# Storing Strassen weight differences from GpSimd, loading two units' partial sums a step earlier, and issuing the first loads from two engines

## The chip, the cores and the metric

The kernel runs on one core of one Trainium2 chip. The metric is the device time of one execution in microseconds; a kernel's time is the median of its timed runs. Besides these there is one profiled execution, from which a trace is taken; its span goes from the first to the last instruction.

## The reference, cut to what matters

One hybrid encoder layer with a final norm, for two sequences with the same weights, "sample" (1024 tokens) and "prompt" (512 tokens), all in float32, model width 2048:

```
h = rms_norm(x, norm_g)
z = h @ w_in                                  # 2048 x 5632
c_val, c_glu, c_gate, q, k, v, a_gate = split(z)
conv_out = silu(layer_norm(depthwise31(c_val * sigmoid(c_glu)))) @ w_pw * silu(c_gate)
attn_out = banded_sink_attention(rope(q), rope(k), v, sink) * silu(a_gate)
x = x + concat(conv_out, attn_out) @ w_out    # 2048 x 2048
y = rms_norm(x, final_norm_g)
```

The change touches how `h @ w_in` begins for the sample, and how `concat(...) @ w_out` is done for the sample. What is computed stays the same.

## The kernel before, in words

**Matrix products.** [...] The two big projections of the sample are made with a Strassen-Winograd scheme: a `Unit` (line 94) makes a 2 x 2 block product from seven block products P1 to P7 instead of eight. Each of the seven is a step of 12 matmuls of 128 x 512 (four blocks of the sum by three passes). Their weight operands are blocks of the raw weights and differences of them, made by VectorE in `make1` and `less2` (lines 145 to 167, through `sub`, line 142). Their token operands are made in the same way from the activations; they are kept in `e.T`. Products gather in three PSUM banks: P6, P7 and P4 go on in the bank of P1, P3 in that of P5. So before P6 starts, the bank's value after P1 has to be taken out (`tap`); the same holds for P7 after P6, for P4 after P7 and for P3 after P5.

**Order of the stages.** The sample's `w_in` products (four groups of units, two halves of the inner dimension each), attention and convolution beside the prompt's `w_in` products (plain `Job`s, line 669), the pointwise products, then the sample's output projection: `over[0]` and `over[1]` (line 2063), eight units of kind `Onto` (line 271) each, for the two halves of the inner dimension. The prompt's end follows (`LastPost`). It makes its output projection by the same scheme with weights and tokens exchanged, and uses the weight differences that the sample's units made: each of the 16 units has `u.sums` (line 1367) and stores its differences P5, P6, P4 (lines 155 to 157) and P7 (lines 165 and 166) to the DRAM arrays `wsum_P5` and so on. Such a store moves 256 KB: 128 partitions of 4 pieces of 512 bytes. The prompt's end reads them back (line 1658).

**Sums in the output projection.** An `Onto` unit adds its products onto a sum that is already in DRAM: the transposed input `xT_s` in `over[0]`, the first half's `part_out` in `over[1]`. `begin` (line 282) takes a buffer with `E()` (line 477: in turn from `g` and `u`, four buffers each) and has SyncE load the sum into it; `tap` (line 301) has VectorE add the PSUM bank onto it at line 304; when the block is complete it is stored, to `part_out` from `over[0]` and to `y_d` (line 1375) from `over[1]`. The four sums are (0,0) for P1, (0,1) for P6, (1,1) for P5 and (1,0) for P4. `product` (line 291) begins the sum of the step that lies `ahead` steps on, and past the last step the (0,0) of the next unit (`self.next`). `open` begins the unit's own (0,0) if nobody has. `ahead` is 2; for the first two units of `over[1]` it is 0 (lines 2088 and 2089), and the first of the two has no `next`.

**Two units side by side.** `grouped` (line 1877) puts the first two units of `over[1]` into one item: `run` (line 640) makes a step of the one and then a step of the other. The second unit (`side`) uses PSUM banks `s`, `s`, `pt`, takes an `a` buffer for its second raw weights, and a `g` buffer for its P6 difference. This lengthens the time in which the token operands of the new half (`switch`, line 1932) are loaded and made.

**What sets the order on an engine.** The program is written in the order of the steps. When it is built, a planner of the framework gives each engine its instructions in a fixed list: it follows the order of the program, with lines under `urgently` or `high_priority` moved forward, and takes what it expects to be ready by estimated times. On the chip each engine and each issuing queue then goes strictly through its list: an instruction that waits holds all behind it. SyncE issues nearly all DMAs: weights (`raw` buffers, three), sums, tokens, and all stores that go through `Encoder.store` (line 503). GpSimd issues only what is written with `nc.gpsimd.dma_start` (lines 268 and 501), and ScalarE eight stores of gates (line 983). DMAs of SyncE go round eight semaphores, so one waits for the eighth before it.

**The head.** `constants` (line 561) has SyncE load `norm_g` first. `first` (line 1886) then loads the first unit's weights in four pieces and the first half of the eight rows `x[k]` of the transposed input in the order of use, and the second halves after that. 20 products of ones (`warm`, line 554) keep TensorE at work until the first operands are there. A row becomes an operand at lines 514 and 515, which need `norm_g`.

Of the kernel before, what the change touches and what calls it, by code (L numbers as in the profile page):

```python
# [7 lines left out]
F32 = mybir.dt.float32  # L8
# [5 lines left out]
P = 128  # L14
D = 2048
ND = D // P
# [17 lines left out]
W = 512  # L34
# [59 lines left out]
class Unit:  # L94
# [50 lines left out]
    def make1(self):  # L145

        if self.late:
            t2 = self.e.G([HALF, P]) if self.side or not self.total else self.e.A([HALF, P], F32)
        else:
            t2 = self.e.PT("p", NP, [HALF, P])  # L150
        r1, r2 = self.r1, self.r2
        self.sub(r1[:, 0], r2[:, 0], r1[:, 0])
        self.sub(t2, r2[:, 1], r1[:, 0])
        self.sub(r1[:, 1], r1[:, 1], t2)
        if self.sums:
            for name, x in (("P5", r1[:, 0]), ("P6", t2), ("P4", r1[:, 1])):
                self.e.store(self.sums[name], x)
        t = self.e.hl_tile()
        for o, x in enumerate((r1[:, 0], t2)):
            self.e.parts(t[:, 0, o], t[:, 1, o], x)  # L160
        return t

    def less2(self):
        self.sub(self.r2[:, 0], self.r2[:, 1], self.r2[:, 0])
        if self.sums:
            self.e.store(self.sums["P7"], self.r2[:, 0])
        self.lessened = True

    def make2(self):
# [261 lines left out]
class Encoder:  # L431
# [129 lines left out]
    def constants(self):  # L561
        nc, a = self.nc, self.a

        def load(key, shape):
            t = self.const.tile([P] + shape, F32, name="c_" + key)
            nc.sync.dma_start(t, a[key])
            return t

        self.norm_g = load("norm_g", [ND])
        self.ones = self.const.tile([P, P], F32, name="ones")  # L570
        nc.vector.memset(self.ones, 1.0)
        self.ones_r = self.const.tile([P, P], F32R, name="ones_r")
        nc.vector.tensor_copy(self.ones_r, self.ones)
        self.norm_n = self.const.tile([P, ND], F32, name="norm_n")

        def rest():
            self.ident = load("ident", [P])
            self.mask = load("mask", [3 * P])
            self.w_dw = load("w_dw", [NC, TAPS])
            self.b_dw = load("b_dw", [NC])  # L580
            self.w_both = self.const.tile([P, NC, (TAPS + 1) // 2], F32, name="w_both")
            nc.vector.tensor_copy(self.w_both[:, :, TAPS // 2 :], self.w_dw[:, :, TAPS - 1 :])
            nc.vector.tensor_tensor(
                self.w_both[:, :, : TAPS // 2], self.w_dw[:, :, 0 : TAPS - 1 : 2], self.w_dw[:, :, 1 : TAPS - 1 : 2], ALU.add
            )
            self.ln_g = load("conv_ln_g", [NC])
            self.ln_b = load("conv_ln_b", [NC])
            self.sink = load("attn_sink", [HEADS])
            self.fin_g = load("final_norm_g", [ND])
            self.stat = {s: self.const.tile([P, TS // P], F32, name=f"stat{s}") for s in (0, 1)}  # L590

        self.more_constants = rest
# [1265 lines left out]
def encoder(ctx, tc, a):  # L1858
    e = Encoder(ctx, tc, a)
    sample, prompt = Sequence(e, 0), Sequence(e, 1)  # L1860
# [24 lines left out]

    def first():
        x = [e.F([TS]) for _ in range(NF)] + [e.A([TS], F32)]
        part = lambda k, t: e.nc.sync.dma_start(x[k][:, t * W : t * W + W], sample.xT[k][:, t * W : t * W + W])
        plain.begin()
        for k in range(2 * HALF):  # L1890
            half, j = divmod(k, HALF)
            if j == 0:
                plain.load_some(0, half, 0, 1)
            part(k, 0)
            if j == 0:
                plain.load_some(1, half, 0, 1)
                plain.load_some(0, half, 1)
            if j == 1:
                plain.load_some(1, half, 1)
        for k in range(2 * HALF):  # L1900
            part(k, 1)
        e.loaded = 2
        e.w_load(3)
        e.warm(20, True)
        sums = sample.first_sums(x)
        x = None
        for half in range(2):
            for j in range(HALF):
                if j == 0:
                    plain.make_some(0, half, 0, 1)  # L1910
                next(sums)
                if j < 2:
                    plain.make_some(1 - j, half, j, HALF if j else 1)
                if j == 1:
                    plain.make_some(1, half, 1)
        e.nc.vector.tensor_scalar(e.norm_n, e.norm_g, -1.0, None, ALU.mult)
        for k in range(2 * HALF):
            next(sums)
        e.ready = 2
        plain.after[3] = [lambda: next(sums)]  # L1920
        plain.after[5] = [lambda: e.T.pop("A21")]
        second = stages[0][2]
        for step in (0, 2, 3):
            second.after.setdefault(step, []).append(lambda: next(sums, None))
        second.after[4] = [e.more_constants]
        second.after.setdefault(6, []).append(lambda: setattr(e, "calm", False))

    for u in stages[0][1:3]:
        u.order = TURNS
    plain.before.append(first)  # L1930

    def switch(unit, nxt, g, seq):
# [153 lines left out]
        u.next = v  # L2086
    jobs += grouped(over[0], None) + grouped(over[1], e.A)
    for u in over[1][:2]:
        u.ahead = 0
    over[1][0].next = None  # L2090
    fj[-1].before.append(lambda: chain[0].begin((0, 0)))

# [67 lines left out]
```

## Time and profile before

| | us |
|---|---|
| three timed runs | 2084.57, 2084.76, 2086.94 |
| median | 2084.76 |
| profiled execution | 2080.18 |
| its span | 2078.4 |
| TensorE busy, matmuls (PE) | 2060.7 |
| VectorE busy (DVE) | 1754.4 |
| ScalarE busy (ACT) | 1043.6 |
| GpSimd busy (POOL) | 122.6 |

How to read it: times in a timeline count from the start of the span. PE is the matmul side of TensorE and PEld its weight loads, DVE is VectorE, ACT ScalarE, POOL GpSimd; SPq, ACTq and POOLq are the queues from which SyncE, ScalarE and GpSimd issue DMAs. A row of a timeline has start, duration, engine, line, operation, output <- inputs, how many are merged, and in brackets the idle time before it with what ended it. A matmul's end is modelled, so pauses are read from weight loads: one stands ahead of each matmul. A row of windows has, for each engine, busy time and count, then the granted TensorE clock, the DMA share and GB/s. In the page's 40 slices of the span (52 us each) TensorE is at 9 tenths or more in all but the last, and GpSimd is below one tenth from the 18th slice on. The output projection of the sample runs from about 1535 to about 1860 us; the prompt's end follows to 2078.

### The profile page before, as it was taken

To read this page: it belongs to the slowest core of one execution; us is meant where nothing else is said; L and a number is where in the kernel's file an instruction comes from. 1 tells how busy PE (TensorE), PEld (TensorE's weight loads), DVE (VectorE), ACT (ScalarE), POOL (GpSimd) and SP (SyncE) were. 2 spreads that over 40 slices of the span, in tenths; PEclk is the share of its full clock that TensorE was granted. 3 is DMA by queue.
4 is the path that set the end of the run, shared out by engine and by line. 5 is a ranking of instruction groups with operands and counts; after the bars stand their busy time and mean duration, and the time that the engine had idled before them with its cause. 6 is when DMAs were issued, how large, how long until landed. Compare 5 with 4: busy or idle time off the path is not lost.

```text
span 2078.4 us, 27092 instructions
## 1 busy us (share of the span) xinstructions
PE 2060.7 (99%) x9259; PEld 1699.2 (82%) x9259; DVE 1754.4 (84%) x2873; ACT 1043.6 (50%) x1711; POOL 122.6 (6%) x176
## 2 busy tenths in 40 slices
PE   9999999999999999999999999999999999999998
PEld 8888888888888888788888888888888887888886
DVE  8767899998899999999666877767799977998887
ACT  7485445333464434554455777336454343454454
POOL 0111111111111111100000000000000000000000
PEclk9999999999999999999999999999999999999999
DMA  8888886864577767954455555996789899678897
GB/s 288 312 298 256 199 223 221 285 220 160 188 242 192 175 169 183 280 166 156 153 172 187 177 182 183 315 330 234 247 289 300 278 299 293 220 247 298 289 333 277
DMA packets 245819, 494.55 MB, mean 238 GB/s; under 512 B 23600, under 2 KB 84400, under 8 KB 245680
## 3 DMA queue, kind: packets, MB, share of 16 engines
q1 hardware_dynamic: 225136, 445.62, 63.9%
q0 software_dynamic: 19392, 45.10, 9.4%
q10 hardware_dynamic: 1152, 2.10, 0.3%
q8 instruction: 72, 1.18, 0.2%
q14 instruction: 67, 0.55, 0.1%
HBM read 331.77 MB, written 160.96 MB: 237 GB/s over the span
## 4 chain that ended last, share of the span: by engine, by line
PE 48%; DVE 7%; issue 6%; DMA 4%; ACT 2%; POOL 1%; SPq 0%; ACTq 0%; POOLq 0%; DVEq 0%
PE a L669 13%; PE a L207 7%; PE c L669 6%; PE b L669 6%; PE c L207 3%; PE pv L1196 2%; PE a L1835 2%; PE s L1167 2%; PE s L1835 2%; PE b L207 1%; PE pt L1201 1%; DVE hl L511 1%; DVE f L1003 1%; DVE t L511 1%; DVE f L1040 1%
## 5 line engine op out<-in xcount | busy, mean ns | idle before, releaser
L207 PE MATMUL a<-t,hl 128*128 128x512 f32 x2640 | 633.6, 391 | 4.7 <-DVE u L304 3.2
L207 PEld LDWEIGHTS a<-t,hl 128*128 128x128 f32 x2640 | 494.7, 188 | 110.6 <-DVE u L304 3.6
L510 ACT ACTIVATE hl<-raw 128x1024 fp32r<-128x1024 f32 (+3 forms) x334 | 296.1, 890 | 384.5 <-PE c L207 81.6
L511 DVE TENSOR_TENSOR hl<-raw,hl 128x1024 fp32r<-128x1024 f32 (+3 forms) x334 | 338.8, 1015 | 145.8 <-ACT hl L510 144.4
L669 PE MATMUL a<-t,hl 128*128 128x512 f32 x1344 | 328.0, 394 | 0.0
L207 PE MATMUL c<-t,hl 128*128 128x512 f32 x1320 | 319.2, 389 | 0.0
L207 PEld LDWEIGHTS c<-t,hl 128*128 128x128 f32 x1320 | 247.3, 188 | 51.6 <-DVE u L304 0.4
L669 PEld LDWEIGHTS a<-t,hl 128*128 128x128 f32 x1344 | 248.6, 188 | 49.8
L1040 DVE SCALAR_TENSOR_TENSOR f<-f,c_w_dw,f 128x512 f32<-128x512 f32 x248 | 173.9, 750 | 0.3
L669 PE MATMUL b<-t,hl 128*128 128x512 f32 x672 | 164.6, 395 | 2.2 <-DVE hl L511 2.2
L1003 DVE SCALAR_TENSOR_TENSOR f<-f,c_w_dw,f 128x512 f32<-128x512 f32 x232 | 163.7, 748 | 1.2 <-ACT f L998 1.2
L669 PE MATMUL c<-t,hl 128*128 128x512 f32 x672 | 164.2, 393 | 0.3 <-DVE hl L511 0.3
L207 PE MATMUL b<-t,hl 128*128 128x512 f32 x660 | 160.0, 389 | 0.0
L669 PEld LDWEIGHTS b<-t,hl 128*128 128x128 f32 x672 | 126.1, 190 | 28.0 <-DVE hl L511 2.6
L669 PEld LDWEIGHTS c<-t,hl 128*128 128x128 f32 x672 | 124.7, 188 | 25.5 <-DVE hl L511 0.7
L207 PEld LDWEIGHTS b<-t,hl 128*128 128x128 f32 x660 | 123.7, 188 | 25.6
L1032 DVE SCALAR_TENSOR_TENSOR f<-f,w_both,f 128x512 f32<-128x512 f32 x120 | 90.0, 750 | 2.1
L236 ACT ACTIVATE u<-a 128x512 f32<-128x512 f32 x82 | 48.7, 594 | 66.8 <-PE a L207 64.2
L236 ACT ACTIVATE g<-a 128x512 f32<-128x512 f32 x78 | 46.3, 594 | 69.1 <-PE a L207 64.6
L1181 ACT ACTIVATE p<-p,tiny 128x384 f32<-128x384 f32 (+1 forms) x96 | 54.5, 570 | 39.8 <-DVE tiny L1178 27.3
L510 ACT ACTIVATE a<-pt 128x512 fp32r<-128x512 f32 x64 | 37.9, 593 | 66.3 <-PE pt L1201 66.2
L511 DVE TENSOR_TENSOR a<-pt,a 128x512 fp32r<-128x512 f32 x64 | 44.1, 689 | 27.3 <-ACT a L510 26.6
(350 smaller groups left out, 2687.9 us busy)
## 6 DMA issues: line engine op xcount, KB each, us to landing
raw<-w_in SPq DMA_DIRECT2D x170, 512.0 KB, 5.3
raw<-w_out SPq DMA_DIRECT2D x31, 512.0 KB, 5.0
raw<-w_pw SPq DMA_DIRECT2D x24, 512.0 KB, 4.2
wsum_P<-raw SPq DMA_DIRECT2D x47, 256.0 KB, 3.3
raw<-wsum_P SPq DMA_DIRECT2D x18, 512.0 KB, 5.0
f<-x_s SPq DMA_DIRECT2D x16, 512.0 KB, 8.2
g<-wsum_P SPq DMA_DIRECT2D x28, 256.0 KB, 4.2
a<-sum_S SPq DMA_DIRECT2D x24, 256.0 KB, 6.2
```

Of the source, the lines that this page charges most:

```text
L207: nc.tensor.matmul(acc, hl[:, l, o, j, :], toks[j][:, r], start=name in FRESH and j == 0 and q == 0, stop=name in LAST and j == HALF - 1 a ...
L236: nc.scalar.activation(t, bank, AF.Copy)
L510: nc.scalar.activation(hi, x, AF.Copy)
L511: nc.vector.tensor_tensor(lo, x, hi.bitcast(F32), ALU.subtract)
L669: nc.tensor.matmul(job.acc[0], hl[:, l, kk // HALF, kk % HALF, :], r, start=i == 0 and p == 0, stop=i == nk - 1 and p == 2,)
L1003: nc.vector.scalar_tensor_tensor(t, h[:, j : j + T], w(j), t, ALU.mult, ALU.add)
L1032: nc.vector.scalar_tensor_tensor(m0, odd[:, j : j + H], both(j), m0, ALU.mult, ALU.add)
L1040: nc.vector.scalar_tensor_tensor(out, d[:, j : j + H], w(2 * j + k), out if j else m0, ALU.mult, ALU.add)
L1167: nc.tensor.matmul(ps[:, 0:n], qs[:, x, h], k[y][:, keys], start=p == 0, stop=p == 2)
L1181: nc.scalar.activation(p[:, 0:n], p[:, 0:n], AF.Exp, bias=nm[:, h : h + 1], accum_out=l[:, h : h + 1])
L1196: nc.tensor.matmul(pv, v[x][:, vs], pt[:, y], start=i == 0 and p == 0, stop=i == last and p == 2)
L1835: nc.tensor.matmul(acc[t], self.toks[name, m][:, x, i, t * P : (t + 1) * P], parts[i][l].rearrange("p a b -> p (a b)"), start=fresh and fi ...
```

## The change

The edits, in the order of the diff: the stores of the weight differences P5, P6, P4 and P7 are issued by GpSimd instead of SyncE; `norm_g` is no longer loaded in `constants`, where only its tile is made; the first half of the first row and `norm_g` are issued by ScalarE, the row first; 13 products of ones instead of 20 stand at the head; and the first two units of `over[1]` begin their sums one step ahead.

```diff
         if self.sums:
             for name, x in (("P5", r1[:, 0]), ("P6", t2), ("P4", r1[:, 1])):
-                self.e.store(self.sums[name], x)
+                self.e.nc.gpsimd.dma_start(self.sums[name], x)
...
         if self.sums:
-            self.e.store(self.sums["P7"], self.r2[:, 0])
+            self.e.nc.gpsimd.dma_start(self.sums["P7"], self.r2[:, 0])
...
-        self.norm_g = load("norm_g", [ND])
+        self.norm_g = self.const.tile([P, ND], F32, name="c_norm_g")
...
-        part = lambda k, t: e.nc.sync.dma_start(x[k][:, t * W : t * W + W], sample.xT[k][:, t * W : t * W + W])
+        part = lambda k, t, q=e.nc.sync: q.dma_start(x[k][:, t * W : t * W + W], sample.xT[k][:, t * W : t * W + W])
         plain.begin()
+        part(0, 0, e.nc.scalar)
+        e.nc.scalar.dma_start(e.norm_g, a["norm_g"])
         for k in range(2 * HALF):
...
-            part(k, 0)
+            if k:
+                part(k, 0)
...
-        e.warm(20, True)
+        e.warm(13, True)
...
     for u in over[1][:2]:
-        u.ahead = 0
+        u.ahead = 1
     over[1][0].next = None
```

## Prediction

> **What bounds the kernel now.** I read the page's busy shares first, then the waits of TensorE's weight loads, then the timeline where the longest wait stands, then the windows around it, and the head last.
>
> ```profile
> span 2078.4 us, 27092 instructions
> PE 2060.7 (99%) x9259; PEld 1699.2 (82%) x9259; DVE 1754.4 (84%) x2873; ACT 1043.6 (50%) x1711; POOL 122.6 (6%) x176
> ```
> TensorE sets the time. An edit counts only where it shortens a pause of TensorE or its slow start. The profiled execution took 2080.18 us (span 2078.4); the median of the three timed runs is 2084.76, 4.58 more, and nothing here shows where. I take the sum from the trace and subtract it from the median.
>
> ```profile
> PEld a L207 <- DVE u L304: 3.6, 1, 3.6
> ```
> Columns: total us, times, longest. The one long wait in the sample's output projection is a product of line 207 waiting for the addition of line 304, 3.6 us at once. The timeline of the weight loads and the sync queue shows the place:
>
> ```profile
> 1721.75 2.68 PEld L207 LDWEIGHTS c<-t,hl 128*128 128x128 f32 x12
> 1724.47 1.55 PEld L207 LDWEIGHTS pt<-t,hl 128*128 128x128 f32 x7
> ...
> 1729.66 3.71 PEld L207 LDWEIGHTS a<-t,hl 128*128 128x128 f32 x12 [3.65 <-DVE u L304]
> 1733.47 3.11 PEld L207 LDWEIGHTS s<-t,hl 128*128 128x128 f32 x12
> 1736.62 1.09 PEld L207 LDWEIGHTS pt<-t,hl 128*128 128x128 f32 x5
> ```
> Twelve weight loads take 2.72 us (1721.75 to 1724.47), 0.227 each. From 1724.47 to 1736.62 there are 31, worth 7.03; they took 12.15. This place loses **5.1 us**, in two parts: the wait, and a slow stretch behind it.
>
> ```profile
> 1727.54:1730.95 3.41, 1.28 (x6) 1.06 (x7) 2.03 (x4) 1.15 (x2) 0.00 (x0) 1.00 0.70 251
> 1730.95:1734.36 3.41, 3.41 (x10) 2.64 (x9) 3.08 (x6) 0.80 (x2) 0.00 (x0) 0.50 0.92 294
> ```
> The third column from the right is the granted clock: after the pause it is 0.50 for 3.41 us, which costs half of that, 1.7. A shorter pause, of about 0.95 us, has no such window behind it:
>
> ```profile
> 842.00:846.00 4.00, 3.05 (x13) 2.55 (x14) 4.00 (x6) 4.00 (x7) 0.00 (x0) 1.00 0.94 218
> ```
>
> **The change, part by part.**
>
> *Stores and the sum load.* What ended the wait is in the timeline:
>
> ```profile
> 1718.21 0.33 SPq L504 DMA_DIRECT2D part_out<-g  x1
> 1718.81 1.57 SPq L504 DMA_DIRECT2D wsum_P<-raw  x2
> 1720.44 0.55 SPq L878 DMA_DIRECT2D p<-mix_d  x1
> 1721.22 0.39 SPq L504 DMA_DIRECT2D wsum_P<-a  x1
> 1721.67 1.75 SPq L878 DMA_DIRECT2D p<-mix_d  x2
> 1723.46 0.43 SPq L285 DMA_DIRECT2D u<-part_out  x1
> ...
> 1728.92 0.69 DVE L304 TENSOR_TENSOR u<-a,u 128x512 f32<-128x512 f32 x1 [2.85 <-DMA u<-part_out]
> ```
> The sum `u<-part_out` is issued at 1723.46 and the addition starts 5.46 later, at 1728.92; TensorE follows 0.74 behind. The sync queue keeps its order, and three weight-difference stores stand just ahead of the load, blocked in turn on VectorE. Without them the last row that waits for VectorE is `part_out<-g`, done at 1718.54. Three `p` loads follow, 0.55 + 1.75, so the sum goes out near 1720.9, 2.5 earlier, and the addition starts near 1726.4, TensorE near 1727.1. TensorE is free at 1724.47 + 7 x 0.227 = 1726.06, so about 1.05 us of pause is left. By the row of 842 that calls no half clock. Gain 5.1 - 1.05, I take **4.0**. The ends: all 5.1, if the load also lands faster; and 2.0 lost, if the product is placed before `c` and `pt` and loses 4.3 us of cover (5.4 pause + 1.7 clock against 5.1 now).
>
> *Sums one step ahead.* The (0,0) sums that end this wait do not depend on `ahead`: the unit before begins one, `open` the other. What `ahead = 1` moves is the next ones, (0,1), (1,1) and (1,0), by one step of both units, 2 x 2.72 us; and the second unit now begins the sum of the third.
>
> ```profile
> 1734.15 0.69 DVE L304 TENSOR_TENSOR u<-a,u 128x512 f32<-128x512 f32 x1 [0.34 <-PE a L207]
> ```
> The next sum, of P6, ended no wait: its addition followed TensorE. But TensorE was 5.1 us late by then; with that gone, this sum could be the next thing late, and one step ahead (5.4 us) covers it. Alone I take 0. The ends: a loss of 5.4, where an early load waits for a buffer and holds the sync queue (below), and no gain, since line 304 holds up TensorE only in the wait above.
>
> *GpSimd as issuer.* Sixteen units store four differences each: 64 issues. The rows are from the DMA list, from lines 504, 268 and 501, and the landing of line 268's stores:
>
> ```profile
> raw<-w_out SPq DMA_DIRECT2D x31, 512.0 KB, 5.0
> ...
> L504 SPq DMA_DIRECT2D wsum_P<-raw x47: 360/371/874, 1532.7 to 1849.2; - x47
> L268 POOL DMA_DIRECT2D part_q<-g x16: 539/539/553, 409.9 to 547.8; - x16
> L501 POOL DMA_DIRECT2D g<-part_q x16 | 15.1, 943 | 64.0 <-DVE g L257 55.8 <-PE a L207 8.3
> DMA to landing us min/median/max: 2.3/4.3/7.6
> ```
> The sync queue loses 64 x 0.37 = 24 us of issues and the waits before them; only the pause above was on the path, so the rest gains 0. A store of the same 256 KB by GpSimd takes 0.54 us (0.94 with an addition) and lands in a median 4.3 us. These stores have four pieces of 512 B per partition instead of one of 2 KB; no row shows GpSimd with such pieces, so one costs between 0.54 and four times 0.94, 3.8. I take 0.54, the nearest row. GpSimd is idle in this stage and nothing else queues on it there. Who waits is the next load into the same `raw` buffer:
>
> ```profile
> 1623.44 0.68 DVE L143 TENSOR_TENSOR raw<-raw,raw 128x512 f32<-128x512 f32 x1
> ...
> 1632.03 0.37 SPq L127 DMA_DIRECT2D raw<-w_out  x1
> ...
> 1644.44 0.69 DVE L143 TENSOR_TENSOR raw<-raw,raw 128x512 f32<-128x512 f32 x1
> ```
> The first difference is ready at 1624.1, and the third store (P7) must land by 1632.0, 7.9 us later. With g us per store and 3.8 (4.3 - 0.54) behind its issue, it lands after 3g + 3.8: up to g = 1.4 nothing moves. The weights loaded at 1632.03 land 5.0 later and are read at 1644.4, which leaves 7.4 us more, up to g = 3.8, the far end. Cost 0 at both ends.
>
> [...]
>
> *The head.*
>
> ```profile
> 0.74 1.28 ACT L510 ACT_TABLE_LOAD   x1 [0.74 <-PEq L2151]
> 0.74 0.39 SPq L566 DMA_DIRECT2D c_norm_g<-norm_g  x1
> ...
> 1.19 0.42 SPq L325 DMA_DIRECT2D raw<-w_in  x1
> ...
> 1.32 4.34 PEld L559 LDWEIGHTS pt<-ones_r 128*128 128x128 f32 x20 [1.32 <-DVE ones_r L573]
> ...
> 1.66 0.42 SPq L1888 DMA_DIRECT2D f<-xT_s  x1
> 2.12 0.91 SPq L325 DMA_DIRECT2D raw<-w_in  x2
> 2.35 0.18 DVE L1916 TENSOR_SCALAR norm_n<-c_norm_g 128x16 f32<-128x16 f32 x1 [1.08 <-DMA c_norm_g<-norm_g]
> ...
> 3.21 0.31 ACT L510 ACTIVATE hl<-raw 128x128 fp32r<-128x128 f32 x1 [1.19 <-DMA raw<-w_in]
> ...
> 4.67 0.72 ACT L514 ACTIVATE t<-f,c_norm_g 128x512 fp32r<-128x512 f32 x1 [1.15 <-DMA f<-xT_s]
> ...
> 5.54 0.33 PEld L349 LDWEIGHTS a<-t,hl 128*128 128x128 f32 x1
> ```
> ScalarE issues the first rows at about 0.74 instead of 1.66, and all sync issues behind move up by the two removed (1.19 - 0.74 and 2.12 - 1.66): 0.9 us. `norm_g` goes out near 1.15, and its 1.6 us to landing leave it in time. ScalarE's own queue gets two issues ahead of its table load, which was done at 2.02 and is needed at 3.2: covered by 1.2 us. The first real product then starts near 4.6. Thirteen spins of 0.213 end at 4.1, so TensorE idles half a microsecond; the seven removed cost nothing, since the data is the bound.
>
> ```profile
> L349 PEld LDWEIGHTS a<-t,hl x6: 288/333/333, 5.5 to 9.8; 128*128 128x128 f32 x6
> ...
> L349 PEld LDWEIGHTS a<-t,hl 128*128 128x128 f32 x42 | 7.9, 188 | 1.6
> ```
> Until about 10.6 us a load takes 333 ns and products follow each other by 0.427; after that 188 and 0.227. If the full clock still comes at 10.6, starting 0.9 earlier puts two more products before it: 0.9 x 0.227/0.427 = **0.5 us** gained. The ends: 1.7 gained if it comes one 3.41 us window earlier, 1.2 lost (1.7 - 0.5) if one later.
>
> Sum: 4.0 + 0.5 = **4.5 us**. The profile would go from 2080.2 to 2075.7, the median from 2084.76 to **2080.3** (0.22% faster; about 0.2%, 4.2 us, is what a measurement of this kernel can tell from no change).
>
> **The rivals.**
>
> *The pause stays or moves (2084.3, chance 0.22).* The order of TensorE's products is fixed when the program is built, by a plan with estimated times: `pt` is cut after seven of twelve and `a` put there, where the planner expected the sum. If it now expects the sum earlier by as much as it really comes earlier, the product moves up and waits as long. For it: that odd cut. Against it: the stores hold the queue only because each waits for VectorE in a fixed order (1.57 us for the two at 1718.81, of 0.37 each), which a plan need not have foreseen. Only the head's 0.5 is left; with the product ahead of `c`, 2086.3.
>
> *The sync queue is held by a sum that waits for its buffer (2087, chance 0.12).*
>
> ```profile
> SPq L285 <- ACT p L1383: 6.6, 4, 5.8
> ```
> The eight sum buffers (four `g`, four `u`) now hold up to six sums of two units and one difference. Line 285 already holds the queue for up to 5.8 us until a buffer is free (longest wait of four). A load one step early that finds none holds it up to 5.4 longer, and the weight loads behind it have 7.4 of slack (above): 5.8 + 5.4 - 7.4 = 3.8 of pause and 1.7 of half clock, 5.5 lost; 2080.3 + 5.5 = 2085.8, and 2091 if it strikes twice; I name 2087. It decides where a hold passes 7.4 us. Against it: few of today's holds are long (6.6 us in all four).
>
> *GpSimd becomes the bound (above 2095, chance 0.06).* Over g = 3.8 the slack is gone, and each further us costs 3 per unit, 42 over the 14 single units. Against it: 0.54 in the nearest row.
>
> *The full clock comes a window earlier (2079.1, chance 0.12) or later (2082.0, chance 0.07).* Real products fill TensorE more than spins do (four times the columns in 0.427 against 0.213 us), which speaks for earlier; the half microsecond of idling for later. [...] That the head isn't faster at all (table load first in ScalarE's queue, rows issued at 2.02) is inside these.
>
> **How the numbers follow.** The forecast, 2080.3, has the rest, 0.41; its own range is 2079 to 2082. Faster by over 0.2% (below 2080.6): 0.12 of the earlier clock and 0.30 of the forecast, 0.42. Slower by over 0.2% (above 2088.9): 0.07 of the held queue, GpSimd's 0.06 and 0.01 of the moved pause, 0.14. The rest, 0.44, is within. The range that leaves out 2 in 10: 2077 to 2088.
>
> **What would show it.** After: no wait of a weight load on line 304 above 1.5 us near 1727, no half-clock row there, `u<-part_out` issued by 1721, GpSimd's stores at 0.5 to 1 us; the first weight load of line 349 at 4.6 and the 333 ns loads ending near 10.6. Wrong would be: the same 3 us wait at another product; `raw<-w_out` later against its split; stores of several us on GpSimd; 333 ns loads beyond 11 us.

## The result, and the profile after

The changed kernel takes 2120.15 us (median; 2117.82 to 2124.66), the kernel before, run beside it, 2084.76. The ratio is 1.017 (95% interval 1.0154 to 1.0185): **1.7% slower, 35 us**, where 2080.3 was forecast and 2088 was the upper end. The profiled execution took 2117.87.

The head of the page after, and the waits of TensorE's weight loads in the output projection, 1540 to 1870 us (us in total, times, longest):

```profile
span 2116.1 us, 27174 instructions
...
PE 2069.4 (98%) x9252; PEld 1700.2 (80%) x9252; DVE 1752.4 (83%) x2873; ACT 1042.2 (49%) x1711; POOL 170.2 (8%) x240
```
```profile
PEld a L207 <- issue: 13.2, 7, 9.8
PEld c L207 <- DVE u L304: 5.9, 2, 3.0
PEld a L207 <- ACT hl L510: 5.2, 2, 3.3
PEld pv L1196 <- DVE a L511: 4.5, 1, 4.5
```
Before, one wait of 3.6 us stood here; now there are many, on every kind of operand. Nearly all of the loss is in this stage. I measure it from its first weight load to its last (1344 loads of line 207 in each kernel): 331.5 us before, 365.0 after. The first half, `over[0]`, went from 172.0 to 199.0, the second, `over[1]`, from 159.5 to 166.0. That is 33.5 of the 37.7 us by which the two profiled executions differ; 3.3 more lie in the prompt's end behind it, and 0.9 ahead of it.

So something common to all operands is late. It is the sync queue. Its own waits in the same stretch, before and after:

```profile
SPq L127 <- DMA wsum_P<-raw: 8.5, 5, 2.9
```
```profile
SPq L127 <- DMA wsum_P<-raw: 62.1, 13, 8.4
SPq L285 <- DMA wsum_P<-g: 29.8, 8, 6.9
...
SPq L123 <- DMA wsum_P<-raw: 18.7, 5, 4.8
```
Lines 123 and 127 load weights into `raw`, line 285 a sum into `g` or `u`. They wait until a weight difference that lies in that buffer has been stored: 110.6 us in all after, 10.6 before (8.5 of it at line 127). All loads behind them wait too, since the queue keeps its order. The longest pause shows the chain (timeline after: TensorE's weight loads, the sync queue, GpSimd, ScalarE and VectorE):

```profile
1722.09 2.68 PEld L207 LDWEIGHTS c<-t,hl 128*128 128x128 f32 x12
...
1723.14 0.76 POOL L157 DMA_DIRECT2D wsum_P<-raw  x1 [3.17 <-issue]
1723.32 2.17 SPq L878 DMA_DIRECT2D p<-msum_S  x4
1725.59 0.58 SPq L504 DMA_DIRECT2D part_out<-u  x1
1728.40 0.63 ACT L510 ACTIVATE t<-p 128x512 fp32r<-128x512 f32 x1 [10.70 <-DMA p<-msum_S]
1729.29 0.33 SPq L127 DMA_DIRECT2D raw<-w_out  x1
1729.72 4.52 SPq L878 DMA_DIRECT2D a<-msum_S  x7
...
1732.03 1.23 DVE L511 TENSOR_TENSOR hl<-raw,hl 128x1024 fp32r<-128x1024 f32 x1 [10.95 <-ACT hl L510]
...
1733.77 0.68 DVE L304 TENSOR_TENSOR u<-a,u 128x512 f32<-128x512 f32 x1
...
1734.57 2.63 PEld L207 LDWEIGHTS a<-t,hl 128*128 128x128 f32 x7 [9.80 <-issue]
```
Read it from the end. TensorE stands still for 9.8 us. The product that waits is the last step of the old half: it needs its PSUM bank, which the addition of line 304 at 1733.77 frees. That addition has nothing to do with the new half, but it stands in VectorE's list behind weight parts (ScalarE copies an operand's high part at line 510, VectorE subtracts it for the low part at line 511; here at 1732.03, after a wait of 10.95 us for ScalarE), and those stand in ScalarE's list behind the first token sums of the new half (`msum_S`), for which ScalarE waited 10.7 us. The sync queue issued these sums late: at 1723.32, behind a load of line 123 that had waited 2.2 us for a weight difference. After 1726.2 it stood at line 127 until 1729.29, because the weights go into a buffer whose difference GpSimd stored only at 1723.14. GpSimd itself was idle for 3.17 us before that store, with nothing that the profile shows to wait for. That idle time is the question. A pause of this length costs a second time: from 3 us after its start the clock is at 0.50 for three times 3.41 us. Only the last of the three falls on products, and costs half of that, 1.7 us:

```profile
1727.73:1737.97 10.24, 3.37 (x8) 2.72 (x9) 5.94 (x9) 6.33 (x10) 0.76 (x1) 0.50 1.02 356
```

GpSimd's stores of one unit in the changed kernel (timeline), and the row of line 157's stores out of `raw` with the landing of all that line 157 issues:

```profile
1560.57 0.75 POOL L157 DMA_DIRECT2D wsum_P<-raw  x1 [12.19 <-DVE tiny L1186]
1565.66 0.76 POOL L157 DMA_DIRECT2D wsum_P<-g  x1 [4.34 <-DVE a L511]
1570.09 0.75 POOL L166 DMA_DIRECT2D wsum_P<-raw  x1 [3.67 <-DVE f L1003]
1574.46 0.76 POOL L157 DMA_DIRECT2D wsum_P<-raw  x1 [3.62 <-DVE hl L511]
```
```profile
L157 POOL DMA_DIRECT2D wsum_P<-raw x32: 752/757/797, 1534.1 to 1895.0; - x32
...
DMA to landing us min/median/max: 2.7/4.5/7.1
```
A store takes 0.76 us to issue, but the four of a unit are 4 to 5 us apart, though VectorE had ended the four subtractions by 1563.3. The releasers in the brackets (a convolution, an attention statistic) have nothing to do with the stores; that is how the profile shows a wait that it can't see. The trace's records of the packets show what it goes with: the last packet of the store of 1565.66 ends at 1569.38 and the next store goes out at 1570.09; then 1573.74 and 1574.46. In all nine such pairs from 1534 to 1598 the next store follows the last packet of the one before by 0.64 to 0.79 us: no two of these stores are under way together.

### The profile page after: what moved, and what is told of

Its sections match the earlier page's. It is cut to its first block, busy times and chain, and to the rows that moved or that the text cites. A ratio compares the mean times of both kernels' runs of the same rounds, so it can differ in the third digit from the quotient of the medians.

```text
span 2116.1 us, 27174 instructions
## 1 busy us (share of the span) xinstructions
PE 2069.4 (98%) x9252; PEld 1700.2 (80%) x9252; DVE 1752.4 (83%) x2873; ACT 1042.2 (49%) x1711; POOL 170.2 (8%) x240
## 4 chain that ended last, share of the span: by engine, by line
PE 39%; issue 15%; DVE 6%; DMA 5%; POOL 2%; ACT 1%; SPq 0%; POOLq 0%; ACTq 0%; DVEq 0%
PE a L669 13%; PE b L669 6%; PE c L669 6%; PE a L207 2%; PE a L1835 2%; PE pv L1196 2%; PE s L1167 2%; DVE hl L511 1%; PE pt L1201 1%; POOL wsum_P L157 1%; PE s L1835 1%; PE c L207 1%; DMA raw<-w_out 1%; DMA u<-part_q 1%; DVE f L1040 1%
## 5 line engine op out<-in xcount | busy, mean ns | idle before, releaser
L157 POOL DMA_DIRECT2D wsum_P<-raw x32 | 24.3, 758 | 853.0 <-DMA f<-msum_S 670.6
```

The costliest lines, as they stand in the source:

```text
L157: self.e.nc.gpsimd.dma_start(self.sums[name], x)
```

## The experiments

**Theory:** a DMA of GpSimd takes up room, by the number of its pieces, until it has drained; the room, which the kernel's build sets (`dynamic_dma_scratch_size`, 1024 bytes), holds one store of 512 pieces, not two, so that each store waits for the one before; buffers come free late, and the sync queue is held. **Rivals:** VectorE's work holds GpSimd up; the sums one step ahead hold the queue; only one DMA of GpSimd runs at a time, whatever its size. The medians of the kernel before beside these runs were 2085.6 to 2086.2; a ratio is worked out from all runs of both kernels and is not the quotient of the two medians.

| kernel | us | ratio to before (95%) | first half | second half |
|---|---|---|---|---|
| before | 2084.76 | | 172.0 | 159.5 |
| changed | 2120.15 | 1.0170 (1.0154 to 1.0185) | 199.0 | 166.0 |
| stores_back | 2086.50 | 1.0009 (0.9994 to 1.0025) | 174.0 | 158.2 |
| stores_alone | 2116.25 | 1.0152 (1.0119 to 1.0185) | 196.6 | 165.8 |
| room_1152 | 2085.68 | 0.9999 (0.9986 to 1.0012) | 176.4 | 156.1 |
| room_1088 | 2086.49 | one run | 176.6 | 157.5 |
| one_piece_b | 2085.63 | 1.0006 (0.9994 to 1.0018) | 174.4 | 155.9 |
| half_stores | 2092.95 | 1.0046 (1.0024 to 1.0068) | 182.4 | 156.7 |
| ahead_alone | 2085.89 | 0.9997 (0.9985 to 1.0009) | 172.7 | 160.2 |
| row_by_scalar | 2086.90 | 1.0002 (0.9992 to 1.0011) | 173.3 | 159.0 |
| second_half | 2087.24 | 1.0007 (0.9996 to 1.0017) | 173.6 | 159.9 |
| room_plain | 2085.14 | 0.9997 (0.9987 to 1.0007) | 179.1 | 154.9 |
| one_piece_plain | 2085.87 | 0.9997 (0.9988 to 1.0006) | 174.0 | 155.8 |

The halves are from one profiled execution each. The four kernels whose stores all go by SyncE (before, stores_back, ahead_alone, row_by_scalar) show their scatter: 172.0 to 174.0 and 158.2 to 160.2.

**stores_back**, the changed kernel without the stores by GpSimd:

```diff
-                self.e.nc.gpsimd.dma_start(self.sums[name], x)
+                self.e.store(self.sums[name], x)
...
-            self.e.nc.gpsimd.dma_start(self.sums["P7"], self.r2[:, 0])
+            self.e.store(self.sums["P7"], self.r2[:, 0])
```


> The changed kernel with the four stores of each unit back on SyncE; the head's edits and the sums one step ahead stay. Theory (the stores): GpSimd issues the next store only after the packets of the one before have left, 3.0 to 5.9 us apart in the trace of the changed kernel, so the raw and g buffers come free late and SyncE's queue waits for them. Then this kernel loses nothing in the output projection: 2079 to 2086 us, and the sync queue waits for wsum_P<-raw at line 127 about as before (8.5 us in all), not 62.1. Rival (the sums one step ahead hold the sync queue): it stays near 2115, with the waits at line 285 as in the changed kernel.

2086.50, half a microsecond above the expected range and level with the kernel before, and the sync queue's wait is back at its old size:

```profile
SPq L127 <- DMA wsum_P<-raw: 8.6, 5, 2.9
```

**stores_alone**, the kernel before with these two edits the other way round and nothing else:

> The kernel before with only the four stores of each unit moved to GpSimd. Theory (the stores): nearly all of the loss is here, 2112 to 2124 us, with pauses of 2 to 10 us of TensorE spread over the output projection. Rival (the sums one step ahead): 2083 to 2087. If both are needed together, it lies between.

2116.25. The two together leave no doubt which edit costs: the stores alone bring 1.5% of the 1.7%, and without them nothing is lost. The sums ahead are out as the cause.

**room_1152**, the changed kernel with more room for GpSimd's DMAs:

```diff
-    nc = bacc.Bacc("TRN2", ..., dynamic_dma_scratch_size=1024)
+    nc = bacc.Bacc("TRN2", ..., dynamic_dma_scratch_size=1152)
```


> [...] Then two stores go out one right behind the other (0.8 to 1 us apart where both are ready, 3.0 at least in the changed kernel), only the third of a unit waits, and more than half of the 33 us comes back: 2082 to 2100 us. [...]

2085.68: 128 bytes of room bring back the whole loss, with the same instructions in the same order on every engine. That is near the good end of what was expected, 2082. The stores of the unit shown above, and the sync queue's waits:

```profile
1564.57 0.75 POOL L157 DMA_DIRECT2D wsum_P<-raw  x1 [18.07 <-DVE tiny L1186]
1566.50 0.76 POOL L157 DMA_DIRECT2D wsum_P<-g  x1 [1.17 <-DVE g L143]
1569.11 0.75 POOL L166 DMA_DIRECT2D wsum_P<-raw  x1 [1.85 <-DVE a L511]
1570.40 0.76 POOL L157 DMA_DIRECT2D wsum_P<-raw  x1 [0.55 <-DVE f L1003]
```
```profile
SPq L127 <- DMA wsum_P<-raw: 19.4, 8, 5.2
SPq L285 <- DMA wsum_P<-g: 14.5, 6, 4.0
```
The unit's four stores now take 5.8 us from first to last, not 13.9; over the 16 groups of four the mean falls from 13.9 to 6.9. The shortest distance between two stores falls from 3.01 to 0.79. A store still takes 0.75 to issue: the issue was never the price.

VectorE is out as the cause: an issue takes 752 to 797 ns in the changed kernel and 750 to 797 here, and the distance between stores changed with the room while VectorE ran the same 2873 instructions in the same order. Were it VectorE that holds GpSimd up, the shortest distance would have stayed at 3.0 us and the time near 2120. How much room a store takes no trace shows. As an estimate from these two kernels, if every store takes the same, it is more than 512 bytes (two don't go into 1024) and at most 576 (two go into 1152).

**room_1088**, the same with 1088 bytes:

> [...]

Shortest distance 0.79 us, projection 334.2 us, one run of 2086.49. Expected were 0.7 to 1.3 us and 330 to 335 us if two stores fit, and 3.0 and at least 360 if not: they fit. By the same estimate a store takes more than 512 and at most 544 bytes.

**one_piece_b**, 1024 bytes as before, but fewer pieces per store (a form that read the differences back in one load, one_piece, gave no time):

```diff
-        self.wsum_d = {p: dram(f"wsum_{p}", [2 * HALF, W], 2) for p in ("P5", "P6", "P7", "P4")}
+        self.wsum_d = {p: dram(f"wsum_{p}", [W // P, 2 * HALF, P], 2) for p in ("P5", "P6", "P7", "P4")}
...
-                u.sums = {p: d[c][:, HALF * g : HALF * g + HALF, n * P : n * P + P] for ...}
+                u.sums = {p: d[c][:, n, HALF * g : HALF * g + HALF, :] for ...}
...
-                    src = self.wsum_d[name][c][:, 2 * m : 2 * m + 2, :].rearrange("p a (b c) -> p a b c", c=P)
+                    src = self.wsum_d[name][c][:, :, 2 * m : 2 * m + 2, :].rearrange("p b a c -> p a b c")
...
-                e.nc.sync.dma_start(raw, src)
+                if name in self.wsum_d:
+                    for n in range(2):
+                        e.nc.sync.dma_start(raw[:, n], src[:, n])
+                else:
+                    e.nc.sync.dma_start(raw, src)
```


> The changed kernel with 1024 bytes of room as it was, but the stored differences laid out in DRAM so that a store writes one piece of 2 KB per partition instead of four of 512 bytes; the prompt's end reads them back in two loads of 256 KB with pieces of 512 bytes instead of one of 512 KB. [...] The whole 2080 to 2092, with what the smaller reads cost at the prompt's end. Rival (bytes in flight, not pieces: 256 KB at a time are all that GpSimd may have under way): the distance stays at 3.0 us and more, the projection above 355 us.

```profile
1561.35 0.54 POOL L157 DMA_DIRECT2D wsum_P<-raw  x1 [20.17 <-DVE tiny L1186]
1563.32 0.55 POOL L157 DMA_DIRECT2D wsum_P<-g  x1 [1.43 <-DVE g L143]
1563.90 0.54 POOL L166 DMA_DIRECT2D wsum_P<-raw  x1
1564.53 0.54 POOL L157 DMA_DIRECT2D wsum_P<-raw  x1
```
With the same bytes in a quarter of the pieces three stores go out within 1.2 us (1563.32 to 1564.53), none waits for another, and the four of a unit take 3.2 us. Each takes 0.54 us: the price that the prediction took, from a row whose stores have one piece of 2 KB per partition. 2085.63, with all the rest of the change in place. So it is neither VectorE nor bytes under way.

**half_stores**, 1024 bytes and four pieces, but each store cut in two:

```diff
-                self.e.nc.gpsimd.dma_start(self.sums[name], x)
+                for j in (0, 2):
+                    self.e.nc.gpsimd.dma_start(self.sums[name][:, j : j + 2], x[:, j : j + 2])
```
(and the same for P7.)

> The changed kernel with 1024 bytes of room, and each store of a difference split into two of 128 KB (256 pieces of 512 bytes each). [...] Half stores then go out 0.5 to 1 us apart until three are under way, and the rest wait; the four stores of a unit take about 10 to 14 us instead of 17 to 21, so the output projection lies between 332.5 (1152 bytes) and 365.0 us (changed), nearer the first: 333 to 348, and the whole 2085 to 2102. Rival (only one DMA of GpSimd at a time, whatever its size): twice as many stores of half the size at 2.5 us and more each, the projection at 365 us or above.

```profile
1560.78 1.42 POOL L158 DMA_DIRECT2D wsum_P<-raw  x2 [15.16 <-DVE tiny L1188]
1562.71 0.72 POOL L158 DMA_DIRECT2D wsum_P<-g  x1 [0.51 <-DVE g L143]
1564.86 0.72 POOL L158 DMA_DIRECT2D wsum_P<-g  x1 [1.43 <-issue]
1565.58 0.71 POOL L168 DMA_DIRECT2D wsum_P<-raw  x1
```
Three halves go out (two at 1560.78, one at 1562.71) and the fourth, of the same difference as the third, waits. That agrees with the estimate, if half the pieces take half the room: more than 256 and at most 272 bytes each, so three go into 1024 and four don't. (The edit moves the line numbers by one or two: L158 is the line of P5, P6 and P4, L168 that of P7.) The projection takes 339.1 us and the whole 2092.95, both inside what was expected. The stores of a unit take 9.5 us in the mean from first to last, less than the 10 to 14 expected; in the changed kernel they take 9.6 to 18.3, 13.9 in the mean, so the "17 to 21" named beside them was too high. The rival of one DMA at a time is out: the shortest distance is 0.70.

**ahead_alone**, the kernel before with `u.ahead = 1` for the two side-by-side units:

> The kernel before with only the sums of the two side-by-side units begun one step ahead. From the prediction: alone it gives nothing, since the sum that is late there is begun outside of it; its ends were a loss of 5.4 and no gain. Theory: second half of the output projection within 2 us of the kernel before (159.5 us), time within 0.2% (2082 to 2090). Rival (an early load holds the sync queue until a buffer is free): second half 164 or more, waits of line 285 near 1720 to 1760 several us longer.

2085.89, second half 160.2: nothing, as predicted. The pause stays where it was, and as long:

```profile
1735.80 2.29 PEld L207 LDWEIGHTS a<-t,hl 128*128 128x128 f32 x8 [4.38 <-DVE u L304]
```

**row_by_scalar**, the head with `norm_g` first on SyncE (`part` takes the queue as in the change):

```diff
+        part(0, 0, e.nc.scalar)
...
-            part(k, 0)
+            if k:
+                part(k, 0)
...
-        e.warm(20, True)
+        e.warm(15, True)
```


> The kernel before with the first half of the first row issued by ScalarE, norm_g left first on SyncE, and 15 products of ones instead of 20. In the changed kernel norm_g went out behind the row at 1.17 and its reader started at 4.55, so that the first operand waited for norm_g (0.43 us at line 514). Theory (norm_g was the late one): the first weight load of line 349 comes at 4.7 to 5.1 us instead of 5.38 (changed) and 5.54 (before). Rival (the loads of the head are slower when more of them start at once, whoever is first): it stays at 5.3 to 5.6. Either way the time is within 0.2% of before, since 0.5 us is less than a measurement tells; the trace decides.

The changed kernel's head, and this one's (timelines):

```profile
0.73 0.41 ACTq L1888 DMA_DIRECT2D f<-xT_s  x1
...
1.17 0.46 ACTq L1891 DMA_DIRECT2D c_norm_g<-norm_g  x1
...
4.55 0.17 DVE L1919 TENSOR_SCALAR norm_n<-c_norm_g 128x16 f32<-128x16 f32 x1 [3.29 <-DMA c_norm_g<-norm_g]
4.61 0.72 ACT L514 ACTIVATE t<-f,c_norm_g 128x512 fp32r<-128x512 f32 x1 [0.43 <-DMA c_norm_g<-norm_g]
...
5.38 0.29 PEld L349 LDWEIGHTS a<-t,hl 128*128 128x128 f32 x1 [1.22 <-ACT t L514]
```
```profile
0.74 0.39 SPq L566 DMA_DIRECT2D c_norm_g<-norm_g  x1
0.75 0.41 ACTq L1888 DMA_DIRECT2D f<-xT_s  x1
...
3.23 0.17 DVE L1918 TENSOR_SCALAR norm_n<-c_norm_g 128x16 f32<-128x16 f32 x1 [1.97 <-DMA c_norm_g<-norm_g]
3.28 1.28 ACT L514 ACT_TABLE_LOAD   x1 [3.28 <-DMA c_norm_g<-norm_g]
...
5.55 0.29 PEld L349 LDWEIGHTS a<-t,hl 128*128 128x128 f32 x1 [0.95 <-ACT hl L510]
```
The first weight load of line 349 stays at 5.55: the rival. `norm_g` is there 1.6 us after its issue before, 2.5 here, 3.4 in the changed kernel; up to 1 us behind its issue two other loads had been issued before, three here, five in the changed kernel. The test isn't clean: the plan put the row's product ahead of the weights on ScalarE here, and the table load stands behind the wait for `norm_g`, at 3.28. So it shows that no earlier start comes of this, but not by which of the two.

**second_half**, room for 1152 bytes, the stores of `over[0]` by SyncE and those of `over[1]` by GpSimd (`u.by = e.nc.gpsimd if last else e.nc.sync`):

> The changed kernel with 1152 bytes of room, and the first half's eight units store by SyncE as before; only the second half's stores go by GpSimd. With 1152 bytes for all units the first half took 176.4 us (before 172.0) and the second 156.1 (before 159.5). Theory (GpSimd's stores cost where every unit loads its weights alone, and help only at the two side-by-side units, where the sync queue is crowded): first half 171 to 174, second 155 to 158, together 326 to 331 against 331.5, so 2080 to 2084 on the median where the kernel before has 2085 to 2086. Rival (the differences between the halves are scatter of single executions): both halves within 2 us of the kernel before.

The rival: 173.6 and 159.9, 2087.24. The first half is as before, as expected, but the second is not shorter: the pause is there again, for another reason (line 510 instead of 304):

```profile
1728.31 4.07 PEld L207 LDWEIGHTS a<-t,hl 128*128 128x128 f32 x12 [3.69 <-ACT hl L510]
```

**room_plain**, the kernel before with the stores by GpSimd and 1152 bytes:

> The kernel before with the stores by GpSimd and 1152 bytes of room; sums not begun ahead, head as before. The prediction's first step alone. Theory (the stores off the sync queue are what shortens the place at 1724 to 1737; the sums ahead give nothing): second half of the output projection 155 to 157 us as in the changed kernel with 1152 bytes (156.1), against 159.0 to 160.2 in three kernels with the stores on SyncE; first half 172 to 177. Rival (it takes the sums one step ahead too): second half 159 to 161, with the half clock after the pause. The median within 0.2% of before either way.

Second half 154.9, first half 179.1, and 2085.14. The stores alone shorten the place that the prediction looked at, without the sums ahead. But the first half is 2 us longer than the longest that was expected (177), and takes back all that the second gained, in part at its end:

```profile
1714.90 6.93 PEld L207 LDWEIGHTS a<-t,hl 128*128 128x128 f32 x24 [2.25 <-ACT t L510]
```
It is the same product that waits as in the chain above, held up in the same way, but for 2 us and not for 10.

**one_piece_plain**, the kernel before with the stores by GpSimd in one piece per partition and the two loads of one_piece_b:

> The kernel before with the stores by GpSimd in one piece of 2 KB per partition and the reads in two loads of 512-byte pieces; 1024 bytes of room, sums not ahead, head as before. It is the candidate for a version that beats both. If the 3.6 us of the second half (159.5 to 155.9 in the changed kernel with this layout) come without loss elsewhere, 2081 to 2084, 0.1 to 0.2% below before. Rival (the first half and the reads at the prompt's end give it back): 2085 to 2088.

2085.87, ratio 0.9997: the rival. Its projection takes 329.8 us against 331.5, and no run here tells 1.7 us from nothing. No kernel of this study beats the one before.

## Why the prediction was wrong, point by point

**The step that failed is GpSimd as issuer: "I take 0.54, the nearest row" and "Cost 0 at both ends".** The issue was 0.76, inside its bounds. But g, the distance from one store to the next, was taken to be the time of an issue, 3.8 at most (four times 0.94). It is the time until the store before has drained: 3.0 at least, and 4.6 in the mean (221.8 us for the three distances of 16 groups). The landing time, 4.3 median, stood in the prediction's own rows, but was counted once, behind the last store, and not between any two. The nearest row was near in bytes and far in what mattered: its stores have 128 pieces, these 512. The prediction did put the four pieces beside its row, and multiplied the issue by them; it had no thought of a room that they fill.

The price per us of g was about right: "each further us costs 3 per unit, 42 over the 14 single units", past g = 3.8, gives (4.6 - 3.8) x 42 = 34; measured are 33.5. So the rival that came true is "GpSimd becomes the bound", which had a chance of 0.06. That the sums agree is in part luck, and proves less than the runs with more room: the slack behind the price was worked out from a single unit, and the loss is not spread evenly over the units. The first half lost 27.0 us and the second 6.5, and a pause of 9.8 us at the switch of the halves, which that price does not know, is part of it.

**The stores leave the sync queue, gain 4.0: the size is right where GpSimd has the room, the way to it is not.** In one_piece_b the sum of the product that waited is issued at 1693.46, its addition is done 4 us before the product that needs the bank, and that product starts without a wait:

```profile
1693.46 0.69 SPq L285 DMA_DIRECT2D u<-part_out  x1
...
1722.34 0.68 DVE L304 TENSOR_TENSOR u<-a,u 128x512 f32<-128x512 f32 x1
...
1726.93 2.68 PEld L207 LDWEIGHTS a<-t,hl 128*128 128x128 f32 x12
```
The two waits behind it are of 1.0 and 0.85 us, no half clock follows, and the second half is 3.6 us shorter (159.5 to 155.9; 3.4 in room_1152, 4.6 in room_plain). In the changed kernel as it was given, none of it is seen.

The prediction kept both orders and moved the sum by 2.5 us, which left 1.05 us of pause. With the stores gone the planner changed both. The sum now goes out 22.6 us ahead of the first product of the new half (1693.46 against 1716.06), where it went out 12.6 behind it (1723.46 against 1710.87); the load of `u` at 1717.32, nearer to the addition, is for a later sum. And the product `a` stands ahead of `c` and `pt` in every kernel whose second half stores by GpSimd: the case that the prediction put at 2.0 us lost. The rival "the pause stays or moves" (0.22) had that much right; it did not see that the sum would be so early that no product waits for it. That the gain comes near 4.0 is therefore luck in part.

The whole does not keep it. Where two stores fit, the first half grows to 176.4 to 179.1 (172.0 to 174.0 with the stores on SyncE): the next thing late are the sums of the new half's tokens, 13 to 15 us before the place that was looked at. With stores of one piece per partition (one_piece_plain and one_piece_b) it is 174.0 and 174.4, at the edge of the scatter. Which load ahead of the token sums makes them late was read from waits, not tried, and stays open.

**Sums one step ahead, 0: right** (ahead_alone). **The head, 0.5: not seen.** The first product came at 5.38 instead of 5.54, not at 4.6. The step that failed is "its 1.6 us to landing leave it in time": `norm_g`, behind the row, took 3.4 and became what the first operand waits for. Neither rival about the clock's window shows: the full clock came at 10.82 us in the changed kernel and at 10.63 before. Over the 13 traces it came between 8.8 and 11.2 us with the new heads and the old alike, so a single trace could not have told. One sum of that part is off: a window of 3.41 us earlier would have gained 3.41 x (1 - 0.227/0.427) = 1.6 us on top of the 0.5, so 2.1 and not 1.7.

Of the signs that were named, "stores of several us on GpSimd" did not show: they stayed at 0.76. "`raw<-w_out` later against its split" did, as 80.8 us of waits at lines 123 and 127.

## What to carry to other kernels

A DMA moved to GpSimd had two prices here: its issue (0.76 us), which the trace shows, and the room that it takes while under way, which the trace shows only as a distance between stores that ends 0.64 to 0.79 us after the last packet of the one before. Count the pieces (partitions times contiguous runs; 512 a store here, 128 in the row that was taken for it), not the bytes, before a store is moved; if two don't fit, lay the target out in longer runs (one_piece_b, 2120.15 to 2085.63) or give more room (room_1152, to 2085.68). And where stores share buffers with loads, the queue that pays is that of the loads: 110.6 us of waits in the sync queue, against 10.6.

## What the runs showed of the hardware that was not expected

The room for GpSimd's DMAs: two stores of 128 partitions x 4 pieces overlapped with 1088 and with 1152 bytes of it (shortest distance 0.79 us) and not with 1024 (3.01); three half stores overlapped with 1024 (0.70). The wait for room is no busy time of GpSimd and has no releaser of its own in the profile: the 3.17 us ahead of the store of 1723.14 stand as "issue", the 4.34 ahead of that of 1565.66 under a VectorE instruction that has nothing to do with it.

The half clock after a pause keeps to a grid. In the changed kernel its windows in the projection start at 1604.85, 1662.87, 1727.73 and 1840.37, that is 17, 19 and 33 times 3.413 us apart. Whether a pause is followed by one is not decided by its length alone: a pause of 2.25 us in room_plain was, one of 3.96 in stores_back was not (the granted clock is the third column from the right):

```profile
1715.36:1718.77 3.41, 3.41 (x10) 2.67 (x9) 3.02 (x6) 3.33 (x5) 1.51 (x2) 0.51 0.87 255
```
```profile
1733.93:1737.35 3.42, 1.74 (x8) 1.43 (x9) 2.49 (x5) 1.15 (x2) 0.00 (x0) 1.00 0.76 267
```
Of five pauses at this place (3.20 us in row_by_scalar, 3.65 before, 3.69 in second_half, 3.96 in stores_back, 4.38 in ahead_alone) all but that of 3.96 were followed by a half clock. So the prediction's 1.7 us for one are a term that may or may not come.

What goes with it in the traces is how much of a pause falls into one window of the grid. The window ahead of the place had matmuls for 1.28 us before and for 0.94 in ahead_alone, and a half clock followed; the pause of stores_back is cut by the grid into windows with 1.47 and 1.82 us of matmuls, and none followed. Over all 13 traces, up to 1900 us, a half clock followed each of the 17 windows at full clock that had at most 1.41 us of matmuls (by their modelled ends) and none of those that had 1.77 or more; of nine between, it followed four (room_plain's, with 1.56, is one). After 1900 us four windows with 2.7 to 3.0 us were followed too, so this is not the whole rule, and what decides it stays open.
